# Two transformer blocks on one core: per-block expert choice, x stored for gathers two pairs ahead, and 42 places for expert weights

## The chip, the cores and the metric

The kernel runs on one NeuronCore of a Trainium2 chip. The metric is the device time of one execution in microseconds (us); where several executions were taken, their median stands. The core has a matrix engine (TensorE, PE), a vector engine (DVE), a scalar engine (ACT), a general engine (GpSimd, POOL) and a queue engine (SyncE, SP) that issues most transfers; 16 DMA engines move data between the chip's memory (HBM) and the core's buffer. In the rows, PEld is PE's loading of weights, and SPq or POOLq is the queue of an engine at the moment at which it issues a transfer.

## The reference, cut to what matters

The program computes two blocks of a transformer on 512 tokens of 1024 features. The first block and the attention parts of the second are left as they were. What is changed is the end of the second block: the product that closes the cross attention, the choice of experts, and the mixture of 32 experts.

```python
def second_block(x, mem, ...):
    ...
    x = x + memory_cross_attention(hc, m, ..., cross_w_o[l])      # ends in o @ w_o
    hm = rms_norm_2(x, moe_norm_g[l])
    x = x + hierarchical_moe(hm, router_w_group[l], router_b_group[l], router_w_expert[l], ...)

def hierarchical_moe(h, w_group, b_group, w_expert, b_expert, w_gate, w_up, w_down):
    ...
        g_logits = einsum('sd,dg->sg', hr, w_group);  g_prob = softmax(g_logits)
        g_sel = argmax(g_logits + b_group)                       # one of 4 groups
        e_logits = the 8 experts of that group
        _, top_idx = top_k(e_logits + e_bias, 2)                 # two experts of it
        top_p = softmax(e_logits)[top_idx] / their sum
        gate = top_p * g_prob[g_sel]                             # (512, 32), two entries a row
        act = silu(einsum('sd,edf->sef', hr, w_gate)) * einsum('sd,edf->sef', hr, w_up) * gate
        return einsum('sef,efd->sd', act, w_down)
```

Every expert's weights (1024 x 256 twice, and 256 x 1024, in fp32) have to be read from HBM once: 32 experts of 3 MB.

## The kernel before, in words

**The stage.** `moe()` takes the 512 tokens in four blocks of 128 (`tb` 0 to 3, tiles `crossq_U`, called `X.rows(tb)` or `self.xs[tb]`) and the 32 experts in 16 pairs. A pair `p` is the experts `p` and `p + 16`, each with 64 slots, so that one pair fills 128 rows of a matrix product. Tokens that don't fit the slots go through a later path that the shown run doesn't enter.

**The weights as a stream.** The weights of the experts are 192 pieces of 512 KB, 12 a pair (eight of `w_gu`, four of `w_dn`), and SP issues them in one fixed order (`prefetch`, L1765; the last four in halves of 256 KB, L1759). They go into a ring, `self.places`, of 35 buffers that other stages have finished with: 2 `early`, 8 `ew` (`EXTRA = 8`), 4 of the X rows, 2 `misc`, 3 `raw`, 4 `whl`, 4 of U, 4 `whl`, 4 of U. Piece n reuses the place of piece n - 35, so its transfer waits until PE has read that piece.

**Ahead of the pairs.** `out_product` (called at the `cross_w_o` line) forms the closing product block by block; `fin0` and `fin1` add each half of a block to x (L1643, L1652), and `logits` transposes x (L1625), takes the router's product (L1634), multiplies x by the norm's gain row into `wo_tA` (L1639) and stores that to a table `hd` in HBM from ACT's queue (L1640). `select` finds the group and the two experts of two blocks at a time (on DVE, lines 1474 to 1527); it runs for blocks 0 and 1 while the product goes on and for blocks 2 and 3 behind the last logits. `route` turns the choice into slots (`pos`, one-hot `oh`); the place of a token is a small product of the choice `mb` with a triangle `trib` and with ones `onb` (L1535). `pair_collect` gathers the tokens of pair 0 by matrix products with `oh` (L1875).

**The pairs.** For each pair: `pair_up` (32 products, L1896), `flip` of the next pair's tokens (transposes L1781, copies to `xT` L1782, one half on DVE, one on ACT), `pair_turn` (transposes of the activation, L1907, copy to `aT` L1909), `pair_take` (one-hot L1795, look-up products L1819 and L1823, and `fetch`, an indirect gather of the tokens of pair i + 3 from `hd` into `moe_xg`, POOL, L1834), `pair_down` (16 products, L1922, two copies into `yt`, L1928) and `pair_scatter` (indirect write of `yt` to `rows`, POOL, L1932). `xg` and `yt` have two buffers each. `pair_last` reads the rows back (L1964), adds them to x and stores the result.

**What sets the order.** A scheduler places the instructions on each engine by dependences and by the order in which the code is written; each engine then works strictly in its own order, so an instruction that waits holds all behind it on that engine.

Of the kernel before, what the change touches and what calls it, by code (L numbers as in the profile page):

```python
# [19 lines left out]
P = 128  # L20
# [8 lines left out]
class Halves:  # L29


    def __init__(self, t):
        self.t = t
# [8 lines left out]
    def rows(self, i):  # L42

        return self.t[i // 4].rearrange("p a b c -> p (a b c)")[:, i % 4 * 1024:(i % 4 + 1) * 1024]


class Kern:
# [1416 lines left out]
    def first_max(self, v, o, mx, mk):  # L1464

        nc = self.nc
        X = mybir.AxisListType.X
        sh = list(v.shape)
        bc = mx.unsqueeze(len(sh) - 1).to_broadcast(sh)
        desc = self.desc[:, :sh[-1]]  # L1470
        for _ in sh[2:]:
            desc = desc.unsqueeze(1)
        k = mk()
        nc.vector.tensor_reduce(mx, v, axis=X, op=ALU.max)
        nc.vector.tensor_tensor(k, v, bc, op=ALU.is_equal)
        nc.vector.tensor_tensor(k, k, desc.to_broadcast(sh), op=ALU.mult)
        nc.vector.tensor_reduce(mx, k, axis=X, op=ALU.max)
        nc.vector.tensor_tensor(o, k, bc, op=ALU.is_equal)

    def soft_exp(self, v, n, scratch):  # L1480

        nc = self.nc
        mx = self.small(4)
        nc.vector.tensor_reduce(mx, v, axis=mybir.AxisListType.X, op=ALU.max)
        t = scratch.tile([P, 4, n], F32, tag=f"r{n}", bufs=6, name=self.nm("se"))
        nc.vector.tensor_tensor(t, v, mx.unsqueeze(2).to_broadcast([P, 4, n]), op=ALU.subtract)
        nc.scalar.activation(t, t, AF.Exp)
        return t

    def dot(self, a, b, n, scratch):  # L1490

        nc = self.nc
        t = scratch.tile([P, 4, n], F32, tag=f"r{n}", bufs=6, name=self.nm("dt"))
        nc.vector.tensor_tensor(t, a, b, op=ALU.mult)
        r = self.small(4)
        nc.vector.tensor_reduce(r, t, axis=mybir.AxisListType.X, op=ALU.add)
        return r

    def select_tiles(self, pm):
        def T(nm, *sh, dt=F32):  # L1500
            return pm.tile([P, 4, *sh], dt, tag=nm, name=nm)

        self.sel = {"oh": T("goh", 4), "o1": T("go1", 4, 8), "o2": T("go2", 4, 8), "mask": T("mask", 32), "mb": T("mb", 32, dt=BF16), "second": T("second", 32, dt=BF16)}
        self.pos = T("pos", 32)

    def select(self, pm, lg, br, t0, n):


        nc = self.nc
        t = slice(t0, t0 + n)  # L1510
        G = lambda: pm.tile([P, n, 4], F32, tag="sg", bufs=4, name=self.nm("sg"))
        E = lambda: pm.tile([P, n, 4, 8], F32, tag="se", bufs=4, name=self.nm("se"))
        s = self.sel
        oh, o1, o2 = s["oh"][:, t], s["o1"][:, t], s["o2"][:, t]
        eb, l3, glb = E(), E(), G()
        nc.vector.tensor_tensor(eb.rearrange("p t g e -> p t (g e)"), lg[:, t, 4:36],
                                br[:, 4:36].unsqueeze(1).to_broadcast([P, n, 32]), op=ALU.add)
        nc.vector.tensor_tensor(glb, lg[:, t, 0:4], br[:, 0:4].unsqueeze(1).to_broadcast([P, n, 4]), op=ALU.add)
        self.first_max(eb, o1, G(), E)
        self.first_max(glb, oh, self.small(n), G)  # L1520
        nc.vector.scalar_tensor_tensor(l3, o1, -1e30, eb, op0=ALU.mult, op1=ALU.add)
        self.first_max(l3, o2, G(), E)
        ob = E()
        nc.vector.tensor_tensor(ob, o1, o2, op=ALU.add)
        ohb = oh.unsqueeze(3).to_broadcast([P, n, 4, 8])
        for dst, v in (("mb", ob), ("mask", ob), ("second", o2)):
            nc.vector.tensor_tensor(s[dst][:, t].rearrange("p t (g e) -> p t g e", g=4), v, ohb, op=ALU.mult)
# [12 lines left out]
    def gates_to(self, gate, pm, lg):  # L1540
# [3 lines left out]
        R = lambda n, nm: pm.tile([P, 4, n], F32, tag=f"r{n}", bufs=6, name=self.nm(nm))  # L1544
        oh = self.sel["oh"]
        ohb = oh.unsqueeze(3).to_broadcast([P, 4, 4, 8])
        gl = lg[:, :, 0:4]

        def of_group(v, nm):

            t = pm.tile([P, 4, 4, 8], F32, tag="r32", bufs=2, name=self.nm(nm))
            nc.vector.tensor_tensor(t, v, ohb, op=ALU.mult)
            r = R(8, nm)
            nc.vector.tensor_reduce(r, t.rearrange("p t g e -> p t e g"), axis=X, op=ALU.add)
            return r
# [640 lines left out]
```

## Time and profile before

| | |
|---|---|
| median of 3 runs | 1535.51 us (1530.5 to 1536.32) |
| the profiled execution | 1530.15 us, of which 1528.4 us are the span from its first to its last instruction |
| busy share of the span | PE 95%, DVE 63%, ACT 44%, POOL 8% |
| moved | 321.66 MB in all |
| the stage of this case | from about 1200 us to the end |

The page's shares are over the whole span, so they don't tell what bounds the last 330 us. For that the rows below take the stage apart: stretches of it with the busy time of each engine and the share of the DMA engines, the chain of waits that ended last, SP's queue, and the order of work on PE and DVE around the first pair.

### The profile page before, as it was taken

What the parts mean: (1) busy time and instruction counts of PE and PEld (TensorE: products, weight loads), DVE (VectorE), ACT (ScalarE), POOL (GpSimd) and SP (SyncE); (2) the same over time, 40 slices, a digit from 0 to 9 for tenths busy, and PEclk for the clock granted to TensorE, in tenths of its full rate; (3) what the DMA queues carried; (4) which work ended last, traced back from release to release, by engine and by line L of the source; (5) the groups of instructions that cost most, each with busy time, mean ns of one, the idle gap of its engine ahead of it and who ended that gap; (6) DMA issues with size and microseconds to landing.
All of it is one profiled execution on the core that took longest, in us unless ns stands there. A gap on an engine that the chain in (4) does not pass through costs nothing.

```text
span 1528.4 us, 19917 instructions
## 1 busy us (share of the span) xinstructions
PE 1459.3 (95%) x7096; PEld 1083.4 (71%) x7096; DVE 958.8 (63%) x2099; ACT 671.2 (44%) x1212; POOL 124.4 (8%) x152
## 2 busy tenths in 40 slices
PE   7989999999999999999999999999999998999886
PEld 5667778778788788888888877878878785333322
DVE  4569999994866866565524778775676557332114
ACT  5553486576755754444324554454354421111010
POOL 0111111111000000000000010000011001111100
PEclk9999999999999999999999999999999999999999
DMA  9899977876376553333425633242343667999997
GB/s 333 308 287 270 272 183 189 225 193 151 111 262 206 179 194 96 97 96 97 145 90 193 200 125 111 93 163 90 97 151 102 232 250 283 416 412 412 409 410 282
DMA packets 95767, 321.66 MB, mean 210 GB/s; under 512 B 13129, under 2 KB 13641, under 8 KB 95664
## 3 DMA queue, kind: packets, MB, share of 16 engines
q1 hardware_dynamic: 80832, 276.39, 51.4%
q0 software_dynamic: 11952, 35.56, 10.5%
q10 hardware_dynamic: 2880, 8.39, 1.4%
q8 instruction: 57, 0.93, 0.2%
q14 instruction: 46, 0.38, 0.1%
HBM read 275.83 MB, written 26.74 MB: 198 GB/s over the span
## 4 chain that ended last, share of the span: by engine, by line
PE 69%; DMA 15%; DVE 9%; ACT 3%; issue 2%; POOL 2%; SPq 0%; ACTq 0%; DVEq 0%; POOLq 0%
PE up_pa L152 5%; PE up_pa L153 5%; PE up_pa L151 5%; PE glu_pa L151 2%; PE glu_pa L152 2%; PE vo_pa L151 2%; PE glu_pa L153 2%; PE vo_pa L153 2%; PE vo_pa L152 2%; PE wout_pa L153 2%; PE wout_pa L151 2%; PE wout_pa L152 2%; DMA wo_U<-in_w_dn_dram 2%; DMA crossq_U<-in_w_gu_dram 2%; DMA moe_U<-in_w_gu_dram 2%
## 5 line engine op out<-in xcount | busy, mean ns | idle before, releaser
L648 DVE SCALAR_TENSOR_TENSOR y<-g,cols,y 128x493 f32<-128x493 f32 (+26 forms) x240 | 165.7, 729 | 5.5 <-ACT y L645 3.8
L152 PE MATMUL up_pa<-u,up_w 128*128 128x512 f32 (+1 forms) x384 | 142.6, 372 | 0.4 <-DVE u L194 0.4
L151 PE MATMUL up_pa<-u,up_w 128*128 128x512 f32 (+1 forms) x384 | 142.3, 372 | 0.3 <-ACT u L193 0.3
L153 PE MATMUL up_pa<-u,up_w 128*128 128x512 f32 (+1 forms) x384 | 142.5, 372 | 0.0
L936 DVE SCALAR_TENSOR_TENSOR up_tA<-up_pa,cols,up_tA 128x511 f32<-128x511 f32 x88 | 65.8, 749 | 72.2 <-ACT up_tA L934 70.8
L151 PEld LDWEIGHTS up_pa<-u,up_w 128*128 128x128 f32 x384 | 72.1, 188 | 13.7 <-ACT u L193 1.1
L152 PEld LDWEIGHTS up_pa<-u,up_w 128*128 128x128 f32 x384 | 72.3, 188 | 13.0 <-DVE u L194 0.6
L153 PEld LDWEIGHTS up_pa<-u,up_w 128*128 128x128 f32 x384 | 72.3, 188 | 12.5
L146 DVE TENSOR_TENSOR down_w<-down_raw,down_w 128x1024 fp32r<-128x1024 f32 x36 | 42.8, 1220 | 55.3 <-ACT down_w L140 55.3
L1782 DVE COPY moe_xT<-moe_pb 128x512 f32<-128x512 f32 x15 | 10.4, 691 | 105.7 <-PE moe_pa L1896 105.3
L146 DVE TENSOR_TENSOR wout_w<-wout_raw,wout_w 128x512 fp32r<-128x512 f32 (+1 forms) x72 | 51.3, 745 | 35.2 <-ACT wout_w L140 35.0
L140 ACT CAST down_w<-down_raw 128x1024 fp32r<-128x1024 f32 x36 | 36.6, 1051 | 64.2 <-PE down_pb L153 33.0
L140 ACT CAST wout_w<-wout_raw 128x512 fp32r<-128x512 f32 (+1 forms) x72 | 44.8, 670 | 44.2 <-PE wout_pa L153 23.7
L934 ACT ACTIVATE up_tA<-up_pa,cols 128x512 f32<-128x512 f32 x44 | 34.4, 781 | 67.8 <-PE up_pa L153 67.7
L1898 ACT ACTIVATE moe_sl<-moe_pa,moe_gt 128x256 f32<-128x256 f32 x16 | 7.6, 474 | 124.1 <-PE moe_pa L1896 124.1
L151 PE MATMUL glu_pa<-mem_U,glu_w 128*128 128x512 f32 x128 | 51.6, 406 | 3.8 <-ACT mem_U L193 3.8
L146 DVE TENSOR_TENSOR up_w<-up_raw,up_w 128x1024 fp32r<-128x1024 f32 (+1 forms) x48 | 54.0, 1127 | 0.1
L152 PE MATMUL glu_pa<-mem_U,glu_w 128*128 128x512 f32 x128 | 51.4, 403 | 0.4 <-DVE mem_U L194 0.4
L152 PE MATMUL g_pa<-g_w,down_U 128*128 128x512 f32 x128 | 51.0, 399 | 0.5 <-DVE g_w L146 0.5
L151 PE MATMUL g_pa<-g_w,down_U 128*128 128x512 f32 x128 | 51.3, 402 | 0.0
L153 PE MATMUL glu_pa<-mem_U,glu_w 128*128 128x512 f32 x128 | 50.8, 398 | 0.0
L153 PE MATMUL g_pa<-g_w,down_U 128*128 128x512 f32 x128 | 50.7, 396 | 0.0
(758 smaller groups left out, 3950.0 us busy)
## 6 DMA issues: line engine op xcount, KB each, us to landing
up_raw<-in_ffn_up_dram SPq DMA_DIRECT2D x44, 512.0 KB
wout_raw<-in_w_out_dram SPq DMA_DIRECT2D x40, 512.0 KB
ew<-in_w_gu_dram SPq DMA_DIRECT2D x39, 512.0 KB
down_raw<-in_ffn_down_dram SPq DMA_DIRECT2D x36, 512.0 KB
glu_U<-in_ada_w_dram SPq DMA_DIRECT2D x32, 512.0 KB
moe_ew<-in_w_gu_dram SPq DMA_DIRECT2D x19, 512.0 KB
mem_raw<-in_w_kv_dram SPq DMA_DIRECT2D x16, 512.0 KB
mem_aw<-in_ada_w_dram SPq DMA_DIRECT2D x16, 512.0 KB
```

Of the source, the lines that this page charges most:

```text
L140: nc.scalar.copy(w[:, 0, c], raw[:, c])
L146: nc.vector.tensor_tensor(w[:, 1, c], raw[:, c], w[:, 0, c].bitcast(F32), op=ALU.subtract)
L151: mm(out, lh, rh, start=start, stop=False)
L152: mm(out, lh, rl, start=False, stop=False)
L153: mm(out, ll, rh, start=False, stop=stop)
L648: nc.vector.scalar_tensor_tensor(acc[:, s:], g[:, :512 - s], cw[:, j:j + 1], acc[:, s:], op0=ALU.mult, op1=ALU.add)
L934: nc.scalar.activation(acc, pq, AF.Identity, scale=cwv(2), bias=self.col("ffn_conv_b", cc))
L936: nc.vector.scalar_tensor_tensor(acc[:, s:], pq[:, :512 - s], cwv(2 - s), acc[:, s:], op0=ALU.mult, op1=ALU.add)
L1782: (nc.scalar.copy if i else nc.vector.tensor_copy)(t[:, i * 4:i * 4 + 4].rearrange("p k c -> p (k c)"), ps)
L1898: nc.scalar.activation(sl, ps[:, :256], AF.Silu, scale=s["gt"][:, 2:3])
```

## The change

Six things are changed, all in `moe()` and what it calls.

1. The ring has 42 places: `EXTRA` is 11, and four places are made of pairs of 512-column buffers (`tA`, `tB`; class `TwoHalves`), each loaded by two transfers of 256 KB whose rows are 2 KB long.
2. x itself is stored to `hd`, from ACT's queue directly behind the add; the gain is multiplied in where the gathered tokens are flipped, so both copies of a flip are now DVE products with the gain. The load of the gain as a row (512 KB) and the eight products of L1639 go.
3. `select` takes one block at a time, one step late (block tb - 1 in `fin1(tb)`, block 3 behind the last logits), with a shorter `first_max` on narrow tiles. `route` and `pair_collect` go block by block too and add up in two PSUM banks; two filler products on PE (L1629, L1637) go.
4. Tokens are gathered two pairs ahead instead of three, into one `xg` buffer; `yt` has one buffer.
5. The gates are computed with fewer DVE operations; those of pairs 1 and 2 come later, and a load of the activation table is called earlier.
6. `iotat` and `back`, used by `pair_last` alone, are made in a free place when pair 15 starts; `pair_last` and the overflow path follow.

```diff
+class TwoHalves:
+    def __init__(self, a, b):
+        self.h = a, b
+    def __getitem__(self, i):
+        p, c = i
+        return self.h[c.start // 512][p, c.start % 512:(c.stop - 1) % 512 + 1]
...
     def first_max(self, v, o):
...
         nc.vector.tensor_reduce(mx, v, axis=X, op=ALU.max)
+        nc.vector.scalar_tensor_tensor(k, v, mx, self.desc[:, :n], op0=ALU.is_equal, op1=ALU.mult)
+        nc.vector.tensor_reduce(m2, k, axis=X, op=ALU.max)
+        nc.vector.tensor_scalar(o, k, m2, None, op0=ALU.is_equal)
...
+    def select(self, pm, tb, eb):
...
+        self.first_max(eb[:, 0:4], oh)
+        nc.vector.tensor_scalar(gm, oh, 1e30, -1e30, op0=ALU.mult, op1=ALU.add)
+        nc.vector.tensor_tensor(g8(v), g8(eb[:, 4:36]), gm.unsqueeze(2).to_broadcast([P, 4, 8]), op=ALU.add)
+        self.first_max(v, o1)
+        nc.vector.scalar_tensor_tensor(v2, o1, -1e30, v, op0=ALU.mult, op1=ALU.add)
+        self.first_max(v2, s["second"][:, tb])
+        for dst in ("mb", "mask"):
+            nc.vector.tensor_tensor(s[dst][:, tb], o1, s["second"][:, tb], op=ALU.add)
...
             x = self.xs[tb][:, c]
+            nc.scalar.dma_start(self.hd[tb * P:(tb + 1) * P, c], x)
...
-            if tb == 3 and h == 1:
-                for _ in range(1):
-                    nc.tensor.matmul(dd[:, :256], self.ident, x[:, :256], start=True, stop=True)
-            t = self.tA()
-            nc.vector.tensor_tensor(t, x, grow[:, c], op=ALU.mult)
-            nc.scalar.dma_start(self.hd[tb * P:(tb + 1) * P, c], t)
...
         def fin1(tb, bank):
             nc.vector.tensor_tensor(self.xs[tb][:, 512:], self.xs[tb][:, 512:], bank, op=ALU.add)
+            if tb == 2:
+                route((0,))
...
-            if tb == 1:
-                return lambda: self.select(pm, lg, br, 0, 2)
+            if tb:
+                self.select(pm, tb - 1, eb[tb - 1])
...
-        self.select(pm, lg, br, 2, 2)
         self.phase = "moe"
+        with self.tc.issue_after(self.logged.ins):
+            for tb in (1, 2):
+                route((tb,))
+                self.pair_collect(st[0], oh, (tb,))
+            self.select(pm, 3, eb[3])
+            route((3,))
+            self.pair_collect(st[0], oh, (3,))
...
+        for t in (self.tA, self.tB):
+            self.places += [TwoHalves(t(), t()) for _ in range(2)]
         self.prefetch(0)
...
-        yt = pm.tile([P, 2, 1024], F32, tag="y", name="yt")
+        yt = pm.tile([P, 1024], F32, tag="y", name="yt")
...
+            if i == 0:
+                gates(1)
+                nwin = self.more_windows(pm, mb, onb)
-            if i + 3 < 16:
-                p = i + 3
+            if i + 2 < 16:
+                p = i + 2
...
-    EXTRA = 8
+    EXTRA = 11
...
+            if isinstance(t, TwoHalves):
+                for h in range(2):
+                    self.nc.sync.dma_start(t.h[h], src[:, h * 512:(h + 1) * 512])
+            else:
+                self.nc.sync.dma_start(t, src)
...
     def flip(self, src):
...
-            (nc.scalar.copy if i else nc.vector.tensor_copy)(t[:, i * 4:i * 4 + 4].rearrange("p k c -> p (k c)"), ps)
+            g = self.col("moe_norm_g", 4 * i, 4)
+            nc.vector.tensor_tensor(t[:, i * 4:i * 4 + 4], ps.rearrange("p (k c) -> p k c", k=4), g.unsqueeze(2).to_broadcast([P, 4, P]), op=ALU.mult)
...
-        xg = s["xg"] = self.pm.tile([P, 1024], F32, tag="xg", bufs=2, name=self.nm("xg"))
+        xg = s["xg"] = self.pm.tile([P, 1024], F32, tag="xg", name=self.nm("xg"))
...
+    def pair_collect(self, s, oh, tbs, hs=(0, 1)):
...
+                                     oh[tb // 2][:, tb % 2], start=k == tb == 0, stop=k == tb == 3)
+        if tbs[-1] < 3:
+            return
...
+        for k in range(4):
+            nc.scalar.activation(t[:, k], s["ps"][0][:, k * P:(k + 1) * P], AF.Copy, scale=self.col("moe_norm_g", k))
+        g = self.col("moe_norm_g", 4, 4)
+        nc.vector.tensor_tensor(t[:, 4:8], s["ps"][1].rearrange("p (k c) -> p k c", k=4), g.unsqueeze(2).to_broadcast([P, 4, P]), op=ALU.mult)
```

On SP, before the change, this stood between the last loads for the cross product (`wo_raw` from `in_cross_w_o`) and its eighth; all `in_w_gu` and `in_w_dn` rows are pieces of expert weights.

```order
L136 DMA wo_raw_10743<-in_cross_w_o_dram 128x1024
L1765 DMA crossq_U_10374<-in_w_dn_dram 128x1024 x2
L1765 DMA crossq_U_10374<-in_w_gu_dram 128x1024 x2
L212 DMA wo_moe_norm_g_10419<-in_moe_norm_g_dram 128x1024
L212 DMA wo_router_b_10421<-in_router_b_dram 128x36
L1591 DMA wr<-in_router_w_dram 128x288
L1765 DMA ew<-in_w_gu_dram 128x1024 x6
L1765 DMA ew<-in_w_dn_dram 128x1024 x2
L136 DMA wo_raw_10748<-in_cross_w_o_dram 128x1024
```

On SP with the change, the same place; the four halves of `tA` stand directly ahead of the first row.

```order
L1749 DMA crossq_U_10374<-in_w_gu_dram 128x1024 x4
L1747 DMA moe_tB_11122<-in_w_gu_dram 128x512
L1747 DMA moe_tB_11123<-in_w_gu_dram 128x512
L1747 DMA moe_tB_11124<-in_w_gu_dram 128x512
L1747 DMA moe_tB_11125<-in_w_gu_dram 128x512
L223 DMA wo_router_b_10419<-in_router_b_dram 128x36
L1559 DMA wr<-in_router_w_dram 128x288
L1749 DMA ew<-in_w_gu_dram 128x1024 x6
L1749 DMA ew<-in_w_dn_dram 128x1024 x4
L1749 DMA ew<-in_w_gu_dram 128x1024
L147 DMA wo_raw_10739<-in_cross_w_o_dram 128x1024
```

Four pieces in halves and three more `ew` pieces have come in ahead of the eighth load for the cross product, and the gain's row has gone.

On PE, before the change, behind the last matrix products of the cross product (`wo_pa` from `wo_w`): transposes and logits of block 3's second half, then the places and the tokens of blocks 0 and 1.

```order
L153 MATMUL wo_pa_10684<-wo_w_10750,crossq_U_10195 128x512
L1625 MATMUL wo_pb_10947<-ident,crossq_U_10373 128x128 x4
L1629 MATMUL wo_pb_10952<-crossq_U_10373,ident 128x256
L1637 MATMUL wo_pb_10952<-crossq_U_10373,ident 128x256
L1634 MATMUL wo_pb_10956<-wr,wo_hT_10954 128x36 x4
L1535 LDWEIGHTS trib
L1535 MATMUL moe_pb_11020<-mb,trib 128x32
```

On PE with the change, the same place.

```order
L164 MATMUL wo_pa_10675<-wo_w_10741,crossq_U_10195 128x512
L1518 LDWEIGHTS trib
L1518 MATMUL wo_pb_10890<-mb,trib 128x32
L1596 MATMUL wo_pb_10898<-ident,crossq_U_10373 128x128 x4
L1864 MATMUL wo_pa_10972<-wo_oh_10465,crossq_U_10373 128x128 x3
L1603 MATMUL wo_pb_10905<-wr,wo_hT_10903 128x36 x4
L1864 MATMUL wo_pa_10972<-wo_oh_10465,crossq_U_10373 128x128
L1596 MATMUL wo_pb_10971<-ident,crossq_U_10373 128x128 x4
L1864 MATMUL wo_pa_10973<-wo_oh_10465,crossq_U_10373 128x128 x4
L1603 MATMUL wo_pb_10988<-wr,wo_hT_10986 128x36 x4
```

The place product of block 0, which needs DVE's choice `mb` for that block, now stands ahead of the transposes and logits of blocks 2 and 3, and the tokens of block 0 lie between these; the tokens of blocks 1, 2 and 3 follow one by one.

On DVE, before the change, one pair in the middle of the stage, from one copy of a result to the next.

```order
L1928 COPY yt<-moe_pa_11419 128x512
L1782 COPY moe_xT_11465<-moe_pb_11466 128x512
L1899 SCALAR_TENSOR_TENSOR moe_sl_11454<-moe_sl_11454,moe_gt_11227,moe_pa_11437 128x256
L1830 TENSOR_REDUCE moe_sm_11587<-moe_pb_11578 128x1
L1842 TENSOR_REDUCE moe_gt_11595<-moe_pb_11578 128x2
L1832 TENSOR_SCALAR moe_sm_11589<-moe_sm_11587 128x1
L1845 TENSOR_REDUCE moe_gt_11595<-moe_pb_11578 64x1 x2
L1909 COPY moe_aT_11481<-moe_pa_11478 128x256
```

On DVE with the change, the same stretch of a pair.

```order
L1910 COPY yt<-moe_pa_11407 128x512
L1887 SCALAR_TENSOR_TENSOR moe_sl_11442<-moe_sl_11442,moe_gt_11304,moe_pa_11425 128x256
L1773 TENSOR_TENSOR moe_xT_11453<-moe_pb_11454,cols 128x512
L1773 TENSOR_TENSOR moe_xT_11453<-moe_pb_11460,cols 128x512
L1897 COPY moe_aT_11469<-moe_pa_11466 128x256
L1821 TENSOR_REDUCE moe_sm_11482<-moe_pb_11473 128x1
```

Both halves of the flip stand between the activation `sl` and the copy `aT`, and the small reductions of the look-up have moved behind `aT`.

## Rows read from the trace of the kernel before

**Rows 1.** Stretches of the stage: busy time by engine, granted clock, DMA share, GB/s.

```profile
core 0: us, PE busy (x) PEld busy (x) DVE busy (x) ACT busy (x) POOL busy (x), PEclk, DMA share, GB/s
1190.00:1210.00 20.00, 19.90 (x107) 16.53 (x107) 12.90 (x28) 10.62 (x29) 0.57 (x2) 0.98 0.31 118
...
1230.00:1240.00 10.00, 10.00 (x64) 8.82 (x63) 3.19 (x9) 3.43 (x6) 0.00 (x0) 1.00 0.36 115
...
1270.00:1278.00 8.00, 8.00 (x57) 4.57 (x57) 6.49 (x36) 0.34 (x2) 2.06 (x2) 1.00 0.33 101
1278.00:1288.00 10.00, 7.55 (x66) 4.95 (x63) 7.27 (x38) 2.34 (x3) 0.11 (x1) 0.91 1.00 374
1288.00:1294.00 6.00, 6.00 (x33) 2.34 (x33) 5.73 (x25) 0.59 (x1) 2.30 (x2) 0.87 0.53 178
...
1300.00:1500.00 200.00, 182.80 (x883) 68.63 (x881) 48.45 (x163) 21.10 (x42) 25.89 (x25) 1.00 1.02 410
1496.00:1500.00 4.00, 3.91 (x14) 0.99 (x11) 0.00 (x0) 0.00 (x0) 0.00 (x0) 1.00 0.96 338
1286.00:1290.00 4.00, 4.00 (x24) 2.96 (x26) 2.57 (x15) 0.00 (x0) 0.84 (x1) 0.57 0.77 307
```

**Rows 2.** The chain of waits: start, us, what; its first link of weights and what follows the last.

```profile
1297.82 11.26 DMA wo_raw<-in_w_gu_dram
...
1501.31 1.95 PE moe_pa L1896 x6
```

**Rows 3.** PE in order of time: the flips of two later pairs, one after the other.

```profile
1312.20 0.66 PE L1781 MATMUL moe_pb<-ident,moe_xg 128*128 128x128 f32 x4
...
1325.17 0.66 PE L1781 MATMUL moe_pb<-ident,moe_xg 128*128 128x128 f32 x4
```

**Rows 4.** SP's queue in order of time: start us, us, engine, line, transfer.

```profile
1218.99 17.52 SPq L1765 DMA_DIRECT2D wo_raw<-in_w_gu_dram  x3
...
1274.79 0.33 SPq L1765 DMA_DIRECT2D early<-in_w_dn_dram  x1
...
1276.51 14.78 SPq L1765 DMA_DIRECT2D ew<-in_w_gu_dram  x7
1291.38 0.38 SPq L1765 DMA_DIRECT2D ew<-in_w_dn_dram  x1
```

**Rows 5.** PE in order of time around the first pair; idle time before in brackets.

```profile
1268.88 3.84 PE L1875 MATMUL moe_pa<-oh,crossq_U 128*128 128x128 f32 x32 [0.93 <-DVE oh L1795]
...
1272.83 1.94 PE L1896 MATMUL moe_pa<-early,moe_xT 128*64 128x512 f32 x8
...
1283.03 1.06 PE L1781 MATMUL moe_pb<-ident,moe_xg 128*128 128x128 f32 x8 [1.04 <-DMA moe_xg<-hd,moe_sm]
...
1288.42 2.51 PE L1922 MATMUL moe_pa<-ew,moe_aT 128*64 128x512 f32 x8
...
1292.48 1.88 PE L1896 MATMUL moe_pa<-crossq_U,moe_xT 128*64 128x512 f32 x8
```

**Rows 6.** Tile `cs_tB`, the last use of a `tB` buffer in the attention stage.

```profile
L1378 PE MATMUL cs_pb<-ident,cs_tB x32: 270/272/299, 1161.6 to 1202.9; 128*128 128x128 f32 x32
```

**Rows 7.** DVE in order of time: the choice of experts behind the last logits.

```profile
1263.56 0.23 DVE L1516 TENSOR_TENSOR wo_se<-lg,wo_router_b 128x64 f32<-128x64 f32 x1
...
1267.40 0.22 DVE L1527 TENSOR_TENSOR mb<-wo_se,goh 128x64 bf16<-128x64 f32 x1
```

**Rows 8.** From issue to landing of tile `moe_xg` (gather), then of `yt` (scatter).

```profile
DMA to landing us min/median/max: 7.3/7.3/7.3
...
DMA to landing us min/median/max: 6.5/7.1/8.4
```

**Rows 9.** POOL, the gather and the scatter of one of these pairs.

```profile
1314.71 1.02 POOL L1834 DMA_INDIRECT moe_xg<-hd,moe_sm  x1 [6.75 <-DVE moe_aT L1909]
1319.91 1.02 POOL L1932 DMA_INDIRECT rows<-yt,moe_sm  x1 [4.18 <-DVE yt L1928]
```

**Rows 10.** DVE, the copy of a flip in the later of these pairs.

```profile
1325.38 0.69 DVE L1782 COPY moe_xT<-moe_pb 128x512 f32<-128x512 f32 x1 [6.24 <-PE moe_pa L1896]
```

More of the change, by code (lines that the diff above doesn't have):

```diff
@@ L1521, in select @@
[L1521 to L1527, printed above, removed]
+        oh = s["oh"][:, tb]
+        E = lambda: pm.tile([P, 32], F32, tag="se", bufs=4, name=self.nm("se"))
@@ L1587, in moe @@
             self.xs.append(t)
-        grow = self.row(pm, "moe_norm_g", "y")
         br = self.row(pm, "router_b")
@@ L1633, in logits @@
             for k in range(4):
-                nc.tensor.matmul(pl[:, :36], hT[:, k], wr[:, 4 * h + k], start=k == 0, stop=k == 3)
-            if tb == 3 and h == 1:
-                for _ in range(1):
-                    nc.tensor.matmul(dd[:, :256], self.ident, x[:, :256], start=True, stop=True)
-            t = self.tA()
-            nc.vector.tensor_tensor(t, x, grow[:, c], op=ALU.mult)
-            nc.scalar.dma_start(self.hd[tb * P:(tb + 1) * P, c], t)
+                self.logged = nc.tensor.matmul(pl[:, :36], hT[:, k], wr[:, 4 * h + k], start=k == 0, stop=k == 3)
             return ss, pl
@@ L1764, in prefetch, with spare @@
             t = self.places[n % len(self.places)]
-            self.nc.sync.dma_start(t, src)
+            if isinstance(t, TwoHalves):
[3 more added lines that the diff above has]
+                self.nc.sync.dma_start(t, src)
             self.pieces.append(t)
+    def spare(self):
+        n = len(self.places)
+        t = [self.places[(192 + j) % n] for j in range(n)]
+        return [v for v in t if not isinstance(v, TwoHalves)]
     def pair_weights(self, p):
@@ L1909, in pair_turn, with pair_down @@
         s["turned"] = nc.vector.tensor_copy(aT.rearrange("p a b -> p (a b)"), pt[:, :256])
[L1911 removed]
+    def pair_down(self, s, w, hs, out):
         nc, pm = self.nc, self.pm
[L1914 to L1916 removed]
         pd = {h: self.psA() for h in hs}
@@ L1924, in pair_down @@
             c = slice(h * 512, (h + 1) * 512)
-            if out is None:
-                self.split(y[:, 0, c], y[:, 1, c], pd[h])
-            else:
-                (nc.vector.tensor_copy if h and len(hs) == 2 else nc.scalar.copy)(out[:, c], pd[h])
+            (nc.vector.tensor_copy if h and len(hs) == 2 else nc.scalar.copy)(out[:, c], pd[h])
     def pair_scatter(self, s, y):
@@ L1933, in pair_scatter, with pair_back, pair_add @@
                                           in_offset=None, bounds_check=2 * S - 1, oob_is_err=False)
-    def pair_add(self, s, tbs=range(4)):
-        nc, y = self.nc, s["y"]
-        back = self.pair_back(s)
-        for tb in tbs:
+    def pair_back(self, s):
+        self.nc.vector.tensor_scalar(self.back, self.iotat, s["gt"][:, 1:2], None, op0=ALU.is_equal)
+    def pair_add(self, s, y):
+        nc = self.nc
+        self.pair_back(s)
+        for tb in range(4):
             for h in range(2):
@@ L1942, in pair_add @@
                 pc = self.psB()
-                for i in range(2):
-                    nc.tensor.matmul(pc, back[:, tb * P:(tb + 1) * P], y[:, i, c], start=i == 0, stop=i == 1)
+                nc.tensor.matmul(pc, self.back[:, tb * P:(tb + 1) * P], y[:, c], start=True, stop=True)
                 nc.vector.tensor_tensor(self.xs[tb][:, c], self.xs[tb][:, c], pc, op=ALU.add)
-    def pair_back(self, s):
-        if "back" not in s:
-            back = s["back"] = self.p0.tile([P, 512], F32R, tag="tA", bufs=4, name=self.nm("back"))
-            self.nc.vector.tensor_scalar(back, self.iotat, s["gt"][:, 1:2], None, op0=ALU.is_equal)
-        return s["back"]
     def pair_last(self, s, w, y):
         nc, tc = self.nc, self.tc
-        n = len(self.places)
+        spare = self.spare()
         z = {}
@@ L1983, in results @@
                 pc = self.psB()
-                nc.tensor.matmul(pc, back[:, tb * P:(tb + 1) * P], y[:, c], start=True, stop=True)
+                nc.tensor.matmul(pc, self.back[:, tb * P:(tb + 1) * P], y[:, c], start=True, stop=True)
                 add(tb, c, pc)
```

191 lines of the change are left out of this document (70 added, 121 removed).

## The prediction

> **What bounds the kernel now.** I read the stretches first. From 1300 to 1500 us the DMA engines are at 1.02 of their time and move 410 GB/s, while PE, busy for 182.8 of 200 us, has gaps [rows 1]. The chain of waits says the same: from 1297.82 to 1501.31 it runs through 17 transfers of expert weights of about 11.2 us each from issue to landing, with a few short pieces of PE near the end [rows 2]. So the end is set by the stream of 192 pieces: by when it can go on after the last stop, by how many pieces are then left, and by their rate. At 410 GB/s a piece of 524,288 bytes takes 1.28 us. PE alone would be quicker: two flips in a row are 12.97 us apart [rows 3], and 12 pieces take 15.4 us, before the gathers and scatters that share the queues.
>
> The reader should next see where the stream stands still. Once the 35 places are full, it needs a place that pair 0 gives back. Between 1270 and 1278 the share is 0.33 (5.4 us idle), from 1278 to 1288 it is 1.00, and between 1288 and 1294 it is 0.53 (2.8 us idle): 8.2 us in all [rows 1]. SP's queue names the causes: the first reissue, `early`, goes out at 1274.79, just when PE has read the first two pieces (1272.83 plus 1.94), and the piece behind the seven `ew` waits until 1291.38, since pair 0's second product starts only at 1288.42 [rows 4, 5]. Earlier there is free time that nothing can use: 0.31 from 1190 to 1210 and 0.36 from 1230 to 1240, that is 13.8 and 6.4 us idle [rows 1].
>
> **Seven more places.** In the order of the changed kernel the four pieces in halves stand among loads that go out near 1200 and the three `ew` pieces ahead of the eighth load for the cross product, so they fall into these 20 us of free time; seven pieces need 9.0 us. The buffers `tA` and `tB` are free by then: the last reader of `tB` in the attention stage ends by 1203 [rows 6]. Were some pieces late, they would fill the 5.4 us of the first stop instead. The cover is there twice, so I cost the loading at nothing. The stream then has 150 pieces left when it resumes instead of 157: 7 x 1.28 = **-9.0 us**. The free place costs SP nothing: its one long hold, 17.52 us up to the third `raw` piece [rows 4], stays, and behind it only loads that come in before the stop wait.
>
> **Halves.** Of the 150 pieces, 12 go into the `TwoHalves` places, as 24 transfers with rows of 2 KB instead of 4 KB. The nearest row is the end of the stream, where the last pieces are loaded in just this form: 338 GB/s at a share of 0.96 against 410 at 1.02 [rows 1]. Taken as it stands a piece costs 1.55 us, 0.27 more; brought to the same share (338 x 1.02 / 0.96 = 359 GB/s) 1.46 us, 0.18 more. Twelve cost 2.2 to 3.2 us; since the last stretch may also be slow because less is queued there, the lower bound is 0. I take **+2.5 us**. The Trainium skill, DMA: Bandwidth & Descriptors, section Specifications, gives 512 B as the smallest transfer that runs at line rate; by it rows of 2 KB would cost nothing and the sum would be 2.5 us lower. The 338 GB/s speak against it, though that row has other causes mixed in.
>
> **When the stream resumes.** This is the step with the widest bounds, since the head of pair 0 is rebuilt. Before, the choice for two blocks runs from 1263.56 to its `mb` at 1267.40, 3.84 us for 15 steps that wait for one another, 0.26 us each [rows 7]; then come places and `oh`, the collect of 32 products (3.84 us, from 1268.88, and one just like it before), and pair 0 starts at 1272.83 [rows 5]. Now each block has its own chain of 16 such steps on narrower tiles. At 0.24 us a step (an estimate between 0.22, the duration of one such operation [rows 7], and these 0.26) a block takes 3.8 us, and with places, slots and the norm's root between them 4.5. Blocks 1, 2 and 3 go one behind the other on DVE. PE's order makes it worse at the start: the place product of block 0 waits for DVE and holds the transposes and logits of blocks 2 and 3 behind it. I walk the new orders with durations of the same shapes: block 1's choice starts at 1260.8, the last `oh` is ready at 1260.8 + 3 x 4.5 = 1274.3, and of the collect only block 3's share is left, 3.84 / 4 = 0.96, with a look-up of 0.35 behind it. Pair 0 starts near 1275.7, **2.9 us later** than before. With 0.04 us more or less a step (48 steps) it is 4.8 or 1.0.
>
> That moves the first stop: its 5.4 us become 8.3. But the second stop goes. With one `xg` buffer pair 2's flip no longer stands ahead of pair 0's second product; counted from pair 0's start T, the gather of pair 1 is issued near T + 1.1, behind a look-up, lands 7.3 us later [rows 8], and from there to `aT` it is 2.5 us (1312.20 to 1314.71 [rows 3, 9]) and a look-up more: the second product follows at T + 11.1, against T + 15.6 before (1272.83 to 1288.42 [rows 5]). It starts at 1286.8, its first place comes free about 2 us later, and the stream, busy from about 1279 with eight pieces and a gather for 11 us, has no gap. Stops of 8.3 instead of 8.2 us, one gather's bytes more or less: **+0.4 us**, bounds -2 and +3.
>
> **PE's clock in the head.** Before, PE was granted 0.57 of its clock from 1286 to 1290, behind a stretch in which it had been busy for 7.55 of 10 us [rows 1], and eight products took 2.51 us there against 1.88 at 1292.48 [rows 5]. In the new head PE has about 7 us of work in the 17 before pair 0, and the two filler products are gone. If pair 0's first product starts at that level (the lower one, 1.2 GHz), the first place comes free up to 1.9 us later and some more slow products follow: 0 to +4 us. I take **+1.2 us**.
>
> **The rest costs nothing.** A flip's second copy moves from ACT to DVE, so `aT` waits for 0.69 us [rows 10] less what ACT's copy held before: about 0.5 us more a pair, 13.5 instead of 12.97. Pair 1's first product follows 4.1 us behind pair 0's second (1288.42 to 1292.48 [rows 5]), at 1290.9; pair 15's starts 14 x 13.5 later, at 1479.9, and takes some 7 us (four times 1.88 less their overlap), to 1487, while the last pieces land near 1496. The cover is 9 us. The gather two pairs ahead goes out 2.5 us after the flip (1314.71 against 1312.20 [rows 3, 9]) and needs 7.3 us, 9.8 of 13 us; the one `yt` buffer is free 8.4 us after the scatter's issue at worst [rows 8], and the next copy into it comes about 10 us after that issue, a pair less the time of the copies. The eight gain products and the gain's row go from a stretch in which neither ended a wait; x is stored to `hd` earlier. Behind the last piece the order is the same 27 us (1501.31 to the end of the span at 1528.4).
>
> **The sum.** -9.0 + 2.5 + 0.4 + 1.2 = -4.9 us. On the profiled execution, 1530.15, that is 1525.3. The median of the runs shown, 1535.51, lies 5.4 us higher, and two of three runs are up there; against it the sum gives **1530.6**, which is what I forecast. About 0.5%, 7.7 us, can be told from no change, so the forecast itself counts as no change.
>
> **The rivals.**
>
> *Halves cost nothing and PE keeps its clock.* -9.0 + 0.4 = -8.6, with a resume that is 1 or 2 us earlier up to -10.6: 1525 to 1527 against the median, faster by more than the bound. For it: the row behind the price of the halves is mixed, and the trace shows one dip of the clock only. Against it: both prices have a row, and no stretch of before is as idle on PE as the new head. By the 512 B rule of the Trainium skill (DMA: Bandwidth & Descriptors, Specifications) alone the sum would be -7.4, 1528.1. Chance for faster in all: 0.34.
>
> *The gather lands too late for its one buffer.* The slower side. If the indirect gather were queued like the weights, which take 11.2 us from issue [rows 2], the pair would last 2.5 + 11.2 + 0.1 = 13.8 us and still be hidden. PE's chain takes over once pair 15 can't finish its first product before the time of today, 1503.3 (1501.31 plus 1.95): (1503.3 - 7 - 1290.9) / 14 = 14.7 us a pair, a landing of 12.1 us. At 13.5 us it would be 16 us a pair and 1290.9 + 14 x 16 + 7 = 1521.9, 18.6 slower: 1554. The trace's 7.3, under the same load, speaks against it. The same holds for the scatter with its one buffer, 8.4 at worst. Chance 0.07.
>
> *The head is later than worked out.* Each microsecond by which pair 0 starts later than 1275.7 costs one microsecond. At 1280.6 nothing is left of the gain; at 1288.3 the kernel would be slower by the bound. It needs steps of 0.34 us and a low clock together for the first (0.1 x 48 = 4.8), which is possible where PE waits for DVE at each block; 1535 to 1540, mostly no change. Chance for slower by over 0.5% from here 0.09.
>
> *The change doesn't do what it says:* the extra places are not filled early, because their buffers are read late or SP is held ahead of them. With the reader of [rows 6] and the room in the first stop I give it 0.03, within the others; it would leave +2.5 + 0.4 + 1.2, 1539.6.
>
> **How the numbers follow.** The forecast (within 0.5%, 1527.8 to 1543.2) has 0.50, faster 0.34, slower 0.16. The range takes the sum on the profiled execution with all bounds good, 1530.15 - 9.0 - 2 = 1519, and the median with the bad ones, 1535.5 - 9.0 + 3.2 + 3 + 4 = 1536.7, stretched to 1539 for the last two rivals.
>
> **What would show it.** Right: a first reissue near 1277.7 to 1280, no stop between 1286 and 1294, 150 pieces at 1.3 us behind it, the last landing near 1496, and 27 us behind that. The halves: stretches of 300 to 360 GB/s near pieces 80, 122 and 164. Wrong: PE waiting for `moe_xg` in each pair, DVE's `aT` as the wait that ends last, a first reissue after 1281, or the median's 5 us above the profile gone or doubled.

## The result: slower by 1.1%

The changed kernel takes 1549.1 us (median of 4 runs, 1546.2 to 1554.7) against 1534.2 for the kernel before (4 runs): a ratio of 1.0112, with a 95% interval from 1.0094 to 1.0131. The forecast was 1530.6 and the range ended at 1539, 10 us below the measured time. The profiled execution of the changed kernel is one of 1548.39 us with a span of 1546.7.

The stream of weights did what it was changed for. Stretches of the changed kernel; columns as in [rows 1]:

```profile
1268.00:1282.00 14.00, 11.18 (x73) 8.23 (x74) 10.96 (x58) 2.95 (x7) 1.16 (x1) 0.91 0.24 83
1282.00:1290.00 8.00, 7.50 (x60) 3.65 (x56) 6.32 (x26) 0.47 (x1) 0.00 (x0) 1.00 1.00 372
1290.00:1294.00 4.00, 4.00 (x22) 1.36 (x20) 3.77 (x19) 0.58 (x1) 0.63 (x1) 1.00 1.04 405
...
1350.00:1400.00 50.00, 45.95 (x254) 21.01 (x251) 17.02 (x59) 3.65 (x7) 7.64 (x8) 1.00 1.02 411
1400.00:1450.00 50.00, 39.61 (x193) 17.18 (x190) 11.82 (x43) 2.70 (x5) 7.24 (x7) 0.91 1.03 412
1450.00:1500.00 50.00, 37.29 (x160) 14.37 (x161) 10.37 (x33) 3.17 (x6) 4.59 (x5) 0.85 0.92 353
```

There is one stop in place of two: 0.24 of 14 us, 10.6 us idle, and from 1282 on no other. After that the DMA engines run as before until about 1490. But PE, which was the engine with time to spare, is busy for only 37.3 of the last 50 us here, at a clock of 0.85. SP's queue in the same kernel has the first reissue and the last piece:

```profile
1280.33 0.80 SPq L1749 DMA_DIRECT2D early<-in_w_gu_dram  x2
...
1492.62 1.58 SPq L1739 DMA_DIRECT2D wo_ew<-in_w_dn_dram  x2
```

and the last piece in the kernel before:

```profile
1501.33 0.33 SPq L1759 DMA_DIRECT2D wo_raw<-in_w_dn_dram  x1
```

In [rows 4] the first reissue goes out at 1274.79, 5.5 us earlier; yet the last piece now goes out at 1494, where before it went out at 1501.33. So the stream is done 7 us earlier, and the span of the kernel ends 18 us later (1546.7 against 1528.4). The chain of waits of the changed kernel shows what took over, near the end (start, us, what):

```profile
1456.19 6.43 DMA moe_xg<-hd,moe_sm
1462.62 0.04 issue
1462.67 1.97 PE moe_pb L1771 x8
1464.64 9.01 PE moe_pa L1884 x32
...
1476.76 7.33 DMA moe_xg<-hd,moe_sm
1484.09 0.04 issue
1484.14 1.11 PE moe_pb L1771 x4
1485.25 8.92 PE moe_pa L1884 x32
```

Where [rows 2] had weights, there are gathers of tokens: PE waits for `moe_xg` before a flip (L1771), and the first product of the next pair (L1884) stands behind that flip. On PE in order of time, the flips of the changed kernel from 1409 on, with the idle time before each in brackets:

```profile
1409.13 1.09 PE L1771 MATMUL moe_pb<-ident,moe_xg 128*128 128x128 f32 x8
1422.32 1.09 PE L1771 MATMUL moe_pb<-ident,moe_xg 128*128 128x128 f32 x8
1434.15 1.16 PE L1771 MATMUL moe_pb<-ident,moe_xg 128*128 128x128 f32 x5 [3.73 <-DMA moe_xg<-hd,moe_sm]
1437.14 0.84 PE L1771 MATMUL moe_pb<-ident,moe_xg 128*128 128x128 f32 x3
1446.47 1.52 PE L1771 MATMUL moe_pb<-ident,moe_xg 128*128 128x128 f32 x6 [4.64 <-DMA moe_xg<-hd,moe_sm]
1449.81 0.69 PE L1771 MATMUL moe_pb<-ident,moe_xg 128*128 128x128 f32 x2
1462.67 1.97 PE L1771 MATMUL moe_pb<-ident,moe_xg 128*128 128x128 f32 x8 [3.97 <-DMA moe_xg<-hd,moe_sm]
1484.14 1.11 PE L1771 MATMUL moe_pb<-ident,moe_xg 128*128 128x128 f32 x4 [4.59 <-DMA moe_xg<-hd,moe_sm]
```

From pair 3's flip up to 1422 the flips are 13.19 us apart and wait for nothing. Then four flips in a row wait for their tokens, 3.73 + 4.64 + 3.97 + 4.59 = 16.9 us, and some of the products behind run at a low clock: 9.01 and 8.92 us for the 32 products of a pair, which take 6.87 in the pairs ahead of these. The granted clock there is 0.78 from 1464.6 to 1473.6 and 0.79 from 1485.2 to 1494.2. What changed at that point is the place of the flip in PE's order. Of the changed kernel's order on PE, pair 11 (L1907 second product, L1884 first product, L1771 flip; the look-up products between are left out; a row of a product here is two records of the trace, a row of a flip is one):

```
L1907 MATMUL moe_pa_12256<-ew,moe_aT_12225 64x512 x2
L1884 MATMUL moe_pa_12274<-ew,moe_xT_12209 64x512 x4
L1771 MATMUL moe_pb_12303<-ident,moe_xg_12242 128x128 x4
L1771 MATMUL moe_pb_12309<-ident,moe_xg_12242 128x128
L1884 MATMUL moe_pa_12274<-ew,moe_xT_12209 64x512
L1771 MATMUL moe_pb_12309<-ident,moe_xg_12242 128x128 x3
L1884 MATMUL moe_pa_12274<-ew,moe_xT_12209 64x512 x7
L1771 MATMUL moe_pb_12398<-ident,moe_xg_12335 128x128 x4
```

Until pair 10 the flip of the next pair stood behind the 16 rows of the first product. In pair 11 the scheduler has put it behind the fourth, and the flip after that one into the same product; that of pair 14 stands ahead of pair 12's whole first product, and half of that of pair 15 ahead of pair 13's. POOL's gathers in the changed kernel show why that costs time:

```profile
1426.25 1.01 POOL L1825 DMA_INDIRECT moe_xg<-hd,moe_sm  x1 [8.22 <-PE moe_pa L1907]
...
1439.45 1.16 POOL L1825 DMA_INDIRECT moe_xg<-hd,moe_sm  x1 [8.22 <-PE moe_pa L1884]
...
1476.76 1.02 POOL L1825 DMA_INDIRECT moe_xg<-hd,moe_sm  x1 [15.52 <-DVE moe_gt L1838]
```

A gather needs two things: the flip ahead of it must have emptied the one buffer, and DVE must have formed the index of the tokens (L1823) from the look-up, which with gathers two pairs ahead stands only one pair ahead of the flip that uses it. DVE's index for the first and the last of these gathers:

```profile
1425.05 0.15 DVE L1823 TENSOR_SCALAR moe_sm<-moe_sm 128x1 int32<-128x1 f32 x1
...
1475.87 0.15 DVE L1823 TENSOR_SCALAR moe_sm<-moe_sm 128x1 int32<-128x1 f32 x1
```

The gather of pair 12 goes out at 1426.25 and lands near 1434. Its buffer was empty at 1423.4 and its index ready at 1425.2. A flip that stands behind the first product would ask for it at 1435 or later. The one that now stands a quarter of the way in asks for it at 1430.4. For pair 15 the buffer was empty at 1464.6, when the flip of pair 14 was done, but the gather went out only at 1476.76, behind an index ready at 1476.0. So the index is what came last, and the distance of two pairs does more to make the gather late than the one buffer does.

### The profile page after: what moved, and what is told of

It reads as the page before. It is cut to its first block, busy times and chain, and to the rows that moved or that the text cites. A ratio compares the mean times of both kernels' runs of the same rounds, so it can differ in the third digit from the quotient of the medians.

```text
span 1546.7 us, 19866 instructions
## 1 busy us (share of the span) xinstructions
PE 1456.9 (94%) x7088; PEld 1091.4 (71%) x7088; DVE 964.0 (62%) x2113; ACT 662.2 (43%) x1193; POOL 124.6 (8%) x152
## 4 chain that ended last, share of the span: by engine, by line
PE 74%; DVE 9%; DMA 8%; issue 3%; ACT 3%; POOL 2%; SPq 0%; ACTq 0%; POOLq 0%; DVEq 0%
PE moe_pa L1884 7%; PE up_pa L163 5%; PE up_pa L164 5%; PE up_pa L162 5%; PE moe_pa L1907 3%; DMA moe_xg<-hd,moe_sm 2%; DMA glu_raw<-in_w_in_dram 2%; PE vo_pa L162 2%; PE vo_pa L163 2%; PE vo_pa L164 2%; PE wout_pa L164 2%; PE wout_pa L162 2%; PE wout_pa L163 2%; PE qk_pa L164 1%; PE qk_pa L163 1%
## 5 line engine op out<-in xcount | busy, mean ns | idle before, releaser
L1887 DVE SCALAR_TENSOR_TENSOR moe_sl<-moe_sl,moe_gt,moe_pa 128x256 f32<-128x256 f32 x16 | 7.7, 478 | 73.7 <-ACT moe_sl L1886 73.7
```

What stands on the lines that cost most here:

```text
L1887: nc.vector.scalar_tensor_tensor(sl, sl, s["gt"][:, 0:1], ps[:, 256:], op0=ALU.mult, op1=ALU.mult)
```

## Experiments

**The flips held in place.** The theory after the result (A): the early place of four flips, together with the one buffer and the gather two pairs ahead, is the loss. The rivals: (B) one buffer is too late wherever the flip stands; (C) the late head and the halves are the loss. The edit ties the flip behind the last of the 16 rows of the pair's first product (`self.upped` is that row):

```diff
-                self.pair_flip(st[i + 1])
+                with self.tc.issue_after(self.upped.ins):
+                    self.pair_flip(st[i + 1])
```

> The changed kernel, with the flips of the next pair tied behind the last product of the pair's own first product, as they stood for pairs 0 to 9. Theory A (from pair 10 on the transposes of a flip stand inside or ahead of the first product, where the gather into the one buffer has only just been issued, and PE waits for it): the five waits of 3.7 to 4.6 us for moe_xg go, PE is not behind the stream any more, the last w_gu piece lands near 1493.6, and the time is 1522.5, 26 us under the changed kernel and 7.7 under the kernel before (ratio 0.995). Rival B (one buffer is too late wherever the flip stands): PE waits for moe_xg behind the first product instead, 1540 or more. Rival C (the late head and the halves made the loss): unchanged near 1548.

Measured: 1525.9 us (median of 10 runs), ratio to before 0.9971, interval 0.9953 to 0.9989: 23 us under the changed kernel by the medians, 22 by the two ratios, and now a little faster than the kernel before. The expected 1522.5 was 3.4 us too low. Who waited for tile `moe_xg` in the held kernel, and then in the changed one:

```profile
  PE moe_pb L1772: 2.0, 2
  DVE moe_xT L1774: 1.4, 1
```

```profile
  PE moe_pb L1771: 19.3, 5
  PEld moe_pb L1771: 14.9, 3
  DVE moe_xT L1773: 2.0, 1
```

The waits are gone with the same one buffer, the same distance of two pairs, the same head and the same halves; theory A stands, B and C fall. The gather goes out as late as before, 3.9 us behind the start of a flip (1426.22 to 1430.14 in the held kernel), but the next flip now stands at 1439.40, after the tokens have landed. (Counted by the order, the first product with flips in it is that of pair 11, not 10.)

**Two buffers, the order left alone.** The other way to remove the same wait:

```diff
-            if i + 2 < 16:
-                p = i + 2
+            if i + 3 < 16:
+                p = i + 3
...
-        xg = s["xg"] = self.pm.tile([P, 1024], F32, tag="xg", name=self.nm("xg"))
+        xg = s["xg"] = self.pm.tile([P, 1024], F32, tag="xg", bufs=2, name=self.nm("xg"))
...
-    EXTRA = 11
+    EXTRA = 10
```

> The changed kernel with two xg buffers and gathers three pairs ahead, as before the change, and one ew place less (41 places); where the flips stand is left to the scheduler. Theory A: flips may stand early, since their tokens have landed; no wait for moe_xg; 1522.5 plus one piece of 1.3 is 1524. Rival C: near 1548, as the changed kernel.

Measured: 1525.7 us (10 runs), ratio 0.9966, interval 0.9954 to 0.9979. Here the scheduler still puts flips ahead of products, more of them than in the changed kernel, and PE waits once for `moe_xg`, in the first pairs. So neither the early flip nor the late gather costs anything alone; the two together do. Every run with one buffer also gathers two pairs ahead, and every run with two buffers three, so the runs don't take these two apart; that the distance counts more is read from the trace above.

**One buffer and two pairs ahead in the kernel before.** The same part of the change alone, in the kernel before; nothing else is touched but the name under which the logits keep their transposed x.

```diff
-        for p in range(3):
+        for p in range(2):
...
-            if i + 3 < 16:
-                p = i + 3
+            if i + 2 < 16:
+                p = i + 2
...
-        xg = s["xg"] = self.pm.tile([P, 1024], F32, tag="xg", bufs=2, name=self.nm("xg"))
+        xg = s["xg"] = self.pm.tile([P, 1024], F32, tag="xg", name=self.nm("xg"))
```

> The kernel before with one part of the change alone: one xg buffer, gathers two pairs ahead (the transposed x of the logits keeps its two buffers under another name). The scheduler puts the flips of pairs 9 to 14 inside or ahead of the first product, as in the changed kernel. Theory A: PE waits for moe_xg four or five times, 3.5 to 4.6 us each, with a low clock behind them: 12 to 20 us slower than before, 1544 to 1552. Rival (the waits need the late head or the 42 places too): within 3 us of before.

Measured: 1551.4 us (4 runs), ratio 1.0123, interval 1.0101 to 1.0146, 19 us slower by the ratio and 20 by the medians: nearly all that the early flips cost in the changed kernel, without its head, its halves or its places. On PE in order of time:

```profile
1406.78 0.66 PE L1781 MATMUL moe_pb<-ident,moe_xg 128*128 128x128 f32 x2 [5.93 <-DMA moe_xg<-hd,moe_sm]
...
1426.40 1.94 PE L1781 MATMUL moe_pb<-ident,moe_xg 128*128 128x128 f32 x8 [3.64 <-DMA moe_xg<-hd,moe_sm]
1446.60 1.94 PE L1781 MATMUL moe_pb<-ident,moe_xg 128*128 128x128 f32 x8 [3.38 <-DMA moe_xg<-hd,moe_sm]
1467.45 1.94 PE L1781 MATMUL moe_pb<-ident,moe_xg 128*128 128x128 f32 x8 [3.89 <-DMA moe_xg<-hd,moe_sm]
1487.50 1.08 PE L1781 MATMUL moe_pb<-ident,moe_xg 128*128 128x128 f32 x4 [3.28 <-DMA moe_xg<-hd,moe_sm]
```

**What the seven places are worth.** The held kernel with the 35 places of before:

```diff
-        for t in (self.tA, self.tB):
-            self.places += [TwoHalves(t(), t()) for _ in range(2)]
...
-    EXTRA = 11
+    EXTRA = 8
```

> e1 with 35 places as before the change: EXTRA 8 and no places made of halves. Theory (the stream of pieces sets the end once the flips are held, and a place is worth its piece): 7 x 1.28 = 9.0 us more than e1, less what the 12 pieces in halves cost there (0 to 2.5): 1529 to 1531.5. Rival (PE's chain of 13.2 us a pair sets the end, so that places are worth nothing): the time of e1.

Measured: 1533.8 us (10 runs), ratio to before 1.0009, interval 0.9999 to 1.0019: 7.9 us more than the held kernel with 42 places. The measured value lies a little above the expected 1529 to 1531.5, but so does the held kernel against its own 1522.5; the difference is within what was expected.

The head differs by some microseconds between profiled executions, so I also split each span at the start of pair 0. The three columns are the last cross product, pair 0's first product, and from there to the end of the span, all from PE's rows in order of time:

| kernel | last cross product | pair 0 starts | from there to the end |
|---|---|---|---|
| before | 1258.90 | 1272.83 | 255.6 |
| changed | 1258.18 | 1278.37 | 268.3 |
| before, one buffer | 1259.98 | 1273.81 | 276.8 |
| held, 35 places | 1260.96 | 1281.15 | 252.2 |
| held, 42 places | 1261.21 | 1284.46 | 244.1 |
| two buffers, 41 places | 1259.71 | 1281.81 | 244.2 |
| held, 42 places, all in halves | 1260.59 | 1280.77 | 250.9 |
| held, wide choice | 1257.30 | 1273.51 | 243.4 |
| held, wide choice, again | 1256.84 | 1273.10 | 244.2 |
| held, wide choice, fillers | 1260.92 | 1274.34 | 244.2 |

From 35 to 42 places it is 252.2 - 244.1 = 8.1 us. From before to the held kernel with as many places it is 255.6 - 252.2 = 3.4 us, about the second stop of [rows 1], 2.8; that this stop is the cause is not shown by a run of its own.

**What halves cost.** The held kernel with every piece loaded in two transfers:

```diff
-                self.nc.sync.dma_start(t, src)
+                for h in range(2):
+                    c = slice(h * 512, (h + 1) * 512)
+                    self.nc.sync.dma_start(t[:, c], src[:, c])
```

> e1 with every piece loaded by two transfers of 256 KB with rows of 2 KB, not only the 12 in the new places. Price taken in the prediction (0.18 to 0.27 us a piece, from 338 GB/s against 410): 138 more pieces behind the stop cost 25 to 37 us, and the DMA engines move 340 to 360 GB/s between 1300 and 1450. Rival (rows of 2 KB run nearly as fast; in the changed kernel the stretches with such pieces showed 373 and 389 GB/s, mixed): 0 to 11 us more than e1, 390 GB/s or above.

Measured: 1532.6 us (10 runs), ratio 1.0006, interval 0.9988 to 1.0025. Stretches of this kernel, and then of the held kernel:

```profile
1350.00:1400.00 50.00, 45.96 (x254) 21.02 (x251) 17.07 (x59) 3.65 (x7) 8.48 (x8) 1.00 1.04 393
1400.00:1450.00 50.00, 45.54 (x232) 19.41 (x228) 14.01 (x46) 3.77 (x7) 7.58 (x8) 1.00 1.03 380
```

```profile
1350.00:1400.00 50.00, 46.97 (x247) 20.66 (x245) 15.48 (x53) 3.80 (x8) 8.68 (x8) 1.00 1.02 411
1400.00:1450.00 50.00, 45.96 (x254) 21.30 (x255) 17.76 (x60) 4.19 (x8) 8.38 (x8) 1.00 1.03 411
```

393 and 380 GB/s against 411 in these stretches, 388 against 401 over the whole of 1300 to 1500, and 5.4 us by the two ratios to before (1.0006 and 0.9971) or 6.8 by the table. The last four pieces go in halves in every kernel, so it is 134 more pieces and not 138: 0.04 to 0.05 us for each, about a quarter of the 0.18 to 0.27 that I had taken (the intervals of the ratios leave 0.01 to 0.07). By that estimate the 12 pieces of the change cost 0.6 us, not 2.5.

**What the head costs.** The held kernel with the choice, the routing and the collect two blocks at a time again:

```diff
-            if tb:
-                self.select(pm, tb - 1, eb[tb - 1])
+            if tb == 1:
+                return lambda: self.select(pm, 0, eb[0])
...
-            for tb in (1, 2):
-                route((tb,))
-                self.pair_collect(st[0], oh, (tb,))
-            self.select(pm, 3, eb[3])
-            route((3,))
-            self.pair_collect(st[0], oh, (3,))
+            route((0, 1))
+            self.pair_collect(st[0], oh, (0, 1))
+            route((2, 3))
+            self.pair_collect(st[0], oh, (2, 3))
```

> e1 with the choice of experts, the routing and the collect two blocks at a time, as before the change. Theory (pair 0 starts 5.5 us later than before because the four choices run one behind the other on DVE, and every microsecond of it is paid at the end): pair 0 starts near 1274 instead of 1278.4, and the time is 4.4 us under e1, 1518. Rival (the second stop of the stream would have taken the time anyway): the time of e1, within 1 us.

Measured: 1522.1 us (4 runs), ratio 0.9939, interval 0.9921 to 0.9957, 3.8 us under the held kernel. In the table pair 0 starts 16.2 us behind the last cross product instead of 20.2 to 23.3, and the rest of the span stays at 243.4 to 244.2: what the head loses is lost at the end, nearly microsecond for microsecond. Run again beside the next experiment:

> e4 once more, beside e6 on the same chip: 1522, the measure for e6.

Measured: 1519.9 us (6 runs), ratio 0.9928, interval 0.9911 to 0.9945.

**Fillers.** The same, with the two filler products put back beside the last logits:

```diff
+            if tb == 3 and h == 1:
+                dd = self.psB()
+                nc.tensor.matmul(dd[:, :256], self.ident, x[:, :256], start=True, stop=True)
...
+            if tb == 3 and h == 1:
+                nc.tensor.matmul(dd[:, :256], self.ident, x[:, :256], start=True, stop=True)
```

> e4 with the two filler products on PE beside the last logits put back. Theory (in e4 PE was granted 0.62 and 0.70 of its clock between 1260 and 1270, and its head took 16.2 us from the last cross product to pair 0 against 13.9 before; the fillers keep the clock): the head takes 14 to 15 us and the time is 1 to 2.3 us under e4. Rival (two products of 0.6 us change nothing of the clock, or the end is PE's chain of 13.2 us a pair): the time of e4.

Measured: 1519.9 us (6 runs), ratio 0.9924, interval 0.9907 to 0.9941: no difference to its twin. This one is not clean. Stretches of the wide choice without, and then with fillers:

```profile
1260.00:1265.00 5.00, 4.06 (x26) 3.96 (x27) 4.26 (x27) 0.02 (x1) 0.54 (x1) 0.62 0.97 327
1265.00:1270.00 5.00, 4.22 (x29) 4.11 (x28) 2.17 (x9) 0.00 (x0) 0.00 (x0) 0.70 0.81 332
```

```profile
1260.00:1265.00 5.00, 4.04 (x28) 2.96 (x27) 3.95 (x24) 1.20 (x3) 1.08 (x2) 1.00 0.99 295
1265.00:1270.00 5.00, 3.95 (x37) 3.84 (x37) 4.71 (x29) 0.00 (x0) 0.00 (x0) 1.00 0.95 383
```

The granted clock is full with the fillers, and the head takes 13.4 us instead of 16.2 and 16.3. But in that execution the last cross product came 3.6 to 4.1 us later, so that pair 0 started no earlier. Whether that shift belongs to the kernel or to the execution is open: over all kernels of the table the last cross product lies between 1256.8 and 1261.2. Only the time is settled, and it is the same.

## Why the prediction was wrong, point by point

*What bounds the kernel, and the seven places:* right. The stream set the end of before and sets that of the held kernel, whose chain of waits runs through weights from 1426 on. With the choice by two blocks it runs through PE, at 13.2 us a pair, up to 1462 and 1433 in the two executions shown, so little of the room between the two is left there. Seven places measured 8.1 us and were put at 9.0 less the halves, 6.5.

*Halves:* mis-sized. The end of the stream, 338 GB/s in [rows 1], was the wrong row: it holds the last pieces, with little queued behind them, and a full stream of halves moves 380 to 395 in stretches of 50 us. The price was 0.6 us where +2.5 was taken; the lower bound was the better guess. The rule of the Trainium skill quoted there (DMA: Bandwidth & Descriptors, Specifications: line rate from 512 B on) came nearer than my row, though 3 to 8% of the rate did go.

*When the stream resumes, and the clock:* right in kind, short in size. Pair 0 was put at 1275.7 and started at 1278.37. The collect of one block was mis-sized: the 3.84 us of [rows 5] are for two blocks, so one block's share is half of it, not a quarter. On PE in order of time in the changed kernel:

```profile
1260.37 0.18 PE L1518 MATMUL wo_pb<-mb,trib 128*128 128x32 bf16 x1 [1.80 <-DVE mask L1510]
...
1267.63 3.43 PE L1864 MATMUL wo_pa<-wo_oh,crossq_U 128*128 128x128 f32 x16 [0.56 <-DVE wo_oh L1786]
...
1276.31 2.05 PE L1864 MATMUL wo_pa<-wo_oh,crossq_U 128*128 128x128 f32 x16 [0.72 <-DVE wo_oh L1786]
1278.20 0.24 PE L1810 MATMUL moe_pb<-parts,moe_oh 128*128 128x3 bf16 x4
1278.37 1.94 PE L1884 MATMUL moe_pa<-early,moe_xT 128*64 128x512 f32 x8
```

The last collect takes 2.05 us, not 0.96; PE waits 1.80 us for block 0's choice; and one collect took 3.43 us at a granted clock of 0.57 (1267.6 to 1271.0). PE was busy for 12.3 of the 17 us from 1261.6 to 1278.6, where about 7 were reckoned, at a granted clock of 0.90. The second stop went as forecast. Together 10.6 us idle against 8.2 before, +2.4, where +0.4 and +1.2 for the clock were taken. The terms that were summed would have come out at -8.7 + 0.6 + 2.4 = -5.7 us with the sizes measured (-8.7 being the 8.1 and the 0.6 of the halves in it); -4.9 was the forecast, and the held kernel measured -5.7 by its median beside before's 1531.6. By the ratio it is -4.4, with an interval from -7.2 to -1.7, so agreement to a tenth is luck. The base of the forecast was also high: 1535.51 was the median of three runs, and 25 and 17 later runs of the kernel before have medians of 1531.6 and 1531.2.

*The rest costs nothing:* this is the step that failed. It took the flip's place from two pairs in the middle of the stage [rows 3], reckoned 2.5 + 7.3 = 9.8 us from flip to landing against 13 us from flip to flip [rows 8, 9], and let that stand for all pairs. The landing was right (7.2 us in the median after the change). The distance was not the same for all pairs: in pair 11 the next flip stood 12 of 16 rows earlier, 5 us, and of the 13 us some 8 were left, less than the 3.9 us to the issue (1422.32 to 1426.25, where 2.5 was taken) and the 7.2 to the landing together. The overlap that was put at no cost so became four waits of 3.7 to 4.6 us. The order of the changed kernel could be read in full beforehand; I read one pair of it, and one that was typical. In the kernel before flips stand early too, from the first pair on, and there PE waits for `moe_xg` only twice, 2.1 us in all, in the first pair: its tokens are gathered three pairs ahead. Why the scheduler moved the flips of just these pairs is open.

*The rivals:* the one with the gather too late for its one buffer had the right wait and the right victim, at 0.07. Its point of decision was put on the landing (12.1 us), which did not move. The other end of that distance moved, and of that I had no rival. From pair 0's start the loss is 268.3 - 244.1 = 24.2 us. The four waits come to 16.9 and the two sets of slow products to 4.2; 2.2 of the remaining 3 were gone by the flip of pair 3, where the products behind the wait for pair 2's tokens ran at a granted clock of 0.68 (1304.7 to 1310.0).

*What would show it:* "PE waiting for `moe_xg` in each pair" was named as the sign of a wrong forecast; it came in four pairs.

## What to carry to other kernels

When a change takes away a buffer or brings a load nearer to its use, look up where every use stands in the new order, not one of a typical pair: a scheduler may pull work forward, and that is free only as long as its inputs are early as well. Where the slack is small, tie the consumer down or keep the earlier gather with its second buffer; either gave 22 to 23 us back here, and the kernel with 42 places, flips held and the choice by two blocks runs at 0.993 of the kernel before, where the change as it was made runs at 1.011. A serial chain of small vector operations ahead of the first big product was paid nearly in full at the end here, where that product opens the stream of loads.

## What the runs showed of the hardware

In a full queue, transfers of 256 KB with rows of 2 KB ran at 380 to 395 GB/s (388 over 1300 to 1500) where 512 KB with rows of 4 KB ran at up to 411 (401 over the same stretch); the size of the transfer and that of the row were changed together. 338 at the end of the stream was not their rate. Where the four waits of 3.7 to 4.6 us lie, PE's granted clock fell to 0.91 and 0.85 as a mean of 50 us, and 32 products took 9.0 instead of 6.9 us at 0.78 and 0.79. An indirect gather of 512 KB landed 7.2 us behind its issue in the median of the changed kernel, 5.5 to 8.8, where queued weights took about 11.2 [rows 2]. In the head, where PE waits for DVE between short products, the clock was at 0.50 in one stretch of the held kernel:

```profile
1265.00:1270.00 5.00, 5.00 (x25) 5.00 (x25) 2.67 (x17) 1.08 (x3) 0.00 (x0) 0.50 1.01 401
```

That is the lower level, 1.2 GHz, and the head of that execution took 23.3 us where it took 20.2 in three others whose head has the same code.
